# Interleaving two output pairs in the up projections of a two-layer decoder trunk

## The chip, the cores and the metric

One core of a Trainium2 chip runs the whole trunk in one launch. The metric is the device time of an execution in microseconds (us). Engines are named as in the profile: PE is TensorE, PEld its weight load, DVE VectorE, ACT ScalarE, POOL GpSimd, SP SyncE, which issues most DMAs.

## What is computed

A trunk of two layers over 1024 tokens of width 1024, in float32: layer 0 mixes with multi-head latent attention, layer 1 with a chunked gMLP unit. After each mixer comes a squared-ReLU MLP and then a gated per-layer embedding. What the change touches is the MLP and the last embedding step:

```python
hn = rms_norm(h, norm_ffn[i])
h = h + jnp.square(jax.nn.relu(hn @ ffn_w_up[i])) @ ffn_w_down[i]     # 1024 -> 4096 -> 1024
hn = rms_norm(h, norm_ple[i])
h = h + jax.nn.sigmoid(hn @ ple_w_gate[i]) * (p[i] @ ple_w_proj[i])   # gate 1024x1024, proj 256x1024
```

## The kernel before

**Numbers.** Every float32 operand of a matmul is split into a high and a low half (`split`, L110: a cast on ACT, L111, a subtraction on DVE, L112), and a product is three matmuls: high by high, high by low, low by high. All matmuls of the MLP have 512 columns.

**The up projection** (`wino_up`, L402) makes the 4096 output rows in 16 *pairs* of two 128-row blocks, and computes each pair by a Strassen-Winograd scheme over halves: seven products instead of eight, each of 12 matmuls (four k-blocks, three matmuls each), 84 in a pair. The seven products (`PRODUCTS`, L391) are numbered 0 to 6 here. Their left operands are combinations of four quarters of the weights (A12, A11, S1, S2, S4, S3, A22 in this order), made by `wino_weights` (L343): two loads of 512 KB (L350), four sums on DVE (L378 to L385) and seven splits. Their right operands are combinations of the normed input (B21, B11, T1, T2, B22, T3, T4), made by `NormX`; T3 and T4 are made late (L296, L302), inside the first pair.

Product 0 goes to a PSUM bank of its own (`y`), products 1, 3, 5 and 6 to bank `x`, products 2 and 4 to bank `z`; `x` and `z` are the halves of one two-bank tile `f0u4g` (pair 4 of layer 0). Between two products of a pair a bank is read out: copies on ACT (L446, L456, L463) and additions on DVE (L452, L466, L484). The finished half rows are then scaled by the norm's root with the ReLU (DVE, L478, L494, L502) and squared (ACT, L479, L495, L503), and each row of 1024 tokens goes to DRAM (`f_apark`, L522) as one store of 512 KB. In the first pair the three opening products run over k-blocks 0 to 2 before k-block 3, and the norm's sums and roots (L213, L222) are made there.

**What sets the order.** The program is a trace; a tile scheduler orders each engine's queue by trace order and by what it holds to be ready, and puts in the waits. Product 6 of a pair is written after product 0 of the next pair (`last`, L500), and each `prepare(n + 1)` puts one weight of the next pair into the trace. Buffers come from pools: `pr` (4 raw loads), `pw` and `ph` (8 each), `pt` (4), `phn` (32 tiles of 512 columns), `pa` (2 large tiles), `pb` (one of each tag), and PSUM as two two-bank tiles `g` and four banks `o`. A tile whose pool is full waits until an older one was used last, by a store too.

**Around it.** `up_first` (L595) starts the first pair's weights during the last steps of the matmul before it: `wo1` in layer 0, `go3` in layer 1. The down projection (`f0d`, `f1d`) follows the up projection. The last step `ple_out` (L846) goes over four blocks of 256 output columns and eight token blocks: 32 tiles of 30 matmuls with 256 columns each (6 for `p`, 24 for the gate), two transposes of `h` (L892), a sigmoid, a product and a sum (L904 to L906) and a store of 128 KB (L907). Its first weights are loaded inside the down projection's last sweep (`down_sweeps`, L607).

Of the kernel before, what the change touches and what calls it, by code (L numbers as in the profile page):

```python
# [16 lines left out]
P = 128  # L17
# [23 lines left out]
def trunk(ctx: ExitStack, tc: tile.TileContext, I, out):  # L41
# [129 lines left out]
    class Norm:  # L171
# [34 lines left out]
        def halve(self, c):  # L206
            acc = self.acc[:, CS[c]]
            shl = tmp(f"{self.name}{c}_shl", [P, 2, 512], F32R)
            self.last = S.copy(shl[:, 0], acc)
            V.tensor_tensor(shl[:, 1], acc, f32(shl[:, 0]), op=ALU.subtract)  # L210
            self.shl[c] = shl

        def sums(self, c, st):  # L213

            if c not in self.shl:
                self.halve(c)
            shl = self.shl[c]
            mm(st, onesr, shl[:, 0], True, False)
            mm(st, onesr, shl[:, 1], False, True)
            self.st[c] = st  # L220

        def roots(self, *chunks):  # L222
# [5 lines left out]
            for c in chunks:  # L228
# [3 lines left out]
                vr = tmp(f"{self.name}{c}_vr", [P, 2, 512])  # L232
# [27 lines left out]
    class NormX(Norm):  # L260
# [35 lines left out]
        def late_t3(self, q, h):  # L296
            t = tmp(f"{self.name}_{q}t3")[:, :512]
# [45 lines left out]
    def wino_weights(w, n):  # L343

        name = f"wx{cnt[0]}_"
        cnt[0] += 1
        raw = []
        for g in range(2):
            r = pr.tile([P, KT, P], F32, tag="raw", name=f"{name}r{g}")
            nc.sync.dma_start(r, w[:, (2 * n + g) * P:(2 * n + g + 1) * P].rearrange("(k p) f -> p k f", p=P))  # L350
            raw.append(r.rearrange("p (q e) f -> p q e f", e=2))
        quad = {f"A{g + 1}{e + 1}": raw[g][:, :, e, :] for g in range(2) for e in range(2)}
        count = [0]

        def new(what):
            m = 7 * n + count[0]
            count[0] += 1
# [8 lines left out]
        def sums(x):  # L366
            if n == 0 and x == "b":
                s = tmp(f"{name}s{x}", [P, 2, 4, P])
            else:
                pool, tag = (pb, "rb") if n == 0 else (ph, "h")  # L370
                s = pool.tile([P, 2, 4, P], F32, tag=tag, name=f"{name}s{x}")
            return s[:, 0], s[:, 1]

        def steps():
            yield put("A12", quad["A12"])
            yield put("A11", quad["A11"])
            s1, s2 = sums("a")
            V.tensor_tensor(s1, quad["A21"], quad["A22"], op=ALU.add)  # L378
            yield put("S1", s1)
            V.tensor_tensor(s2, s1, quad["A11"], op=ALU.subtract)  # L380
            yield put("S2", s2)
            s4, s3 = sums("b")
            V.tensor_tensor(s4, quad["A12"], s2, op=ALU.subtract)
            yield put("S4", s4)
            V.tensor_tensor(s3, quad["A11"], quad["A21"], op=ALU.subtract)  # L385
            yield put("S3", s3)
            yield put("A22", quad["A22"])

        return steps()

# [11 lines left out]
    def wino_up(w, F, nrm, first, h, nm, out, side):  # L402


        nfp = F // 256
        gens = {0: first[0], 1: wino_weights(w, 1)}
        made = {0: first[1]}

        def prepare(n):
            if n in gens:  # L410
                t = next(gens[n], None)
                if t is not None:
                    made.setdefault(n, []).append(t)

        def scale(u):
            for c in range(2):
                nrm.sums(c, pso(f"{u}st{c}"))
            nrm.roots(0, 1)

        def pair(n, late):  # L420
            u = f"{nm}{n}"
            if n + 2 < nfp:
                gens[n + 2] = wino_weights(w, n + 2)
            wt = made.setdefault(n, [])
            g = psg(f"{u}g")
            bank = {"x": g[:, CS[0]], "z": g[:, CS[1]], "y": pso(f"{u}y")}
            e0 = tmp(f"{u}e", [P, 2, 512])
            row = [tmp(f"{u}a0", [P, 2, 512])]

            def run(i, qs=range(4)):  # L430
                while len(wt) <= i:
                    prepare(n)
                c, b = PRODUCTS[i]
                product_x(bank[b], wt[i], nrm.x[c], i in OPENS, qs)

            if n == 0:
                for qs in (range(3), range(3, 4)):
                    for i in range(3):
                        run(i, qs)
                while len(wt) < 5:  # L440
                    prepare(0)
                for q in range(2):
                    nrm.late_t3(q, h)
            else:
                run(0)
            S.copy(e0[:, 0], bank["y"])  # L446
            if late is not None:
                late()
            prepare(n + 1)
            if n > 0:  # L450
                run(1)
            V.tensor_tensor(row[0][:, 0], bank["x"], e0[:, 0], op=ALU.add)  # L452
            if n > 0:
                prepare(n + 1)
                run(2)
            S.copy(e0[:, 1], bank["z"])  # L456
            if n == 0:
                for q in range(2, 4):
                    nrm.late_t3(q, h)
# [1022 lines left out]
```

## Time and profile before

| what | value |
|---|---|
| median of 3 runs | 2678.71 us (2677.26 to 2680.14) |
| the profiled execution | 2679.63 us, of which its span 2677.9 us |
| instructions | 34086 |
| granted TensorE clock, mean | 0.997 |

The profile is one execution. A row of the timeline has the start and duration in us, the engine, the line, the operation, its output and inputs, a count, and in brackets the idle time before it and what ended it. PE's matmuls are pipelined, so one shows as 0.39 us though the next starts 0.23 us after it. In the view of windows the count in brackets behind an engine's busy time is that of its instructions that touch the stretch.

### The profile page before, as it was taken

How to read it: one execution, taken by the hardware profiler on the slowest of the kernel's cores; microseconds unless marked ns; L12 is line 12 of the kernel's file. 1: busy time of each engine (PE TensorE's matmuls, PEld its weight loads, DVE VectorE, ACT ScalarE, POOL GpSimd, SP SyncE). 2: the span in 40 equal slices, each digit the busy share in tenths (PEclk: the TensorE clock that was granted, in tenths of full speed). 3: DMA queues.
4: the chain of work that ended last, by engine and by line, in shares of the span. 5: the costliest groups of instructions: out<-in, count | busy, mean ns of one | idle time of the engine just before them, and what ended most of it. 6: DMA issues, size and time to landing. Idle time of an engine off the chain costs nothing.

```text
span 2677.9 us, 34086 instructions
## 1 busy us (share of the span) xinstructions
PE 2618.7 (98%) x13216; PEld 2205.9 (82%) x13216; DVE 1479.2 (55%) x2398; ACT 1038.9 (39%) x2095; POOL 324.0 (12%) x460
## 2 busy tenths in 40 slices
PE   7999999999999999999999999999999999999999
PEld 7988888777777888888888787888677778888899
DVE  5777775975555434475522534437865654443642
ACT  4577772653443212164522312315643341221431
POOL 4544430000000000001211423020000000000000
PEclk9999999999999999999999999999999999999999
DMA  5200012242346323233233212212333363332221
GB/s 166 66 12 17 25 40 79 79 141 96 110 143 203 111 70 110 63 99 91 91 105 107 92 45 74 87 48 95 103 103 110 110 211 120 111 110 70 80 68 36
DMA packets 207026, 247.48 MB, mean 92 GB/s; under 512 B 9056, under 2 KB 168352, under 8 KB 206864
## 3 DMA queue, kind: packets, MB, share of 16 engines
q1 hardware_dynamic: 202048, 230.21, 26.4%
q0 software_dynamic: 4816, 15.10, 1.8%
q8 instruction: 104, 1.70, 0.3%
q14 instruction: 58, 0.48, 0.1%
HBM read 186.55 MB, written 58.72 MB: 92 GB/s over the span
## 4 chain that ended last, share of the span: by engine, by line
PE 85%; DVE 6%; ACT 3%; DMA 1%; issue 1%; POOL 0%; DVEq 0%; ACTq 0%; SPq 0%; POOLq 0%
PE f0d L65 13%; PE f1d L65 13%; PE vp L65 7%; PE go L65 6%; PE up L65 6%; PE e L65 4%; PE pg L65 3%; PE wo L65 3%; PE s L65 2%; PE pq L65 1%; PE av L65 1%; PE pj L65 1%; PE sv L65 1%; PE pk L65 1%; PE f1u9g L400 1%
## 5 line engine op out<-in xcount | busy, mean ns | idle before, releaser
L111 ACT CAST wh<-raw 128x1024 fp32r<-128x1024 f32 x96 | 101.0, 1052 | 386.1 <-PE f1d L65 135.1
L584 DVE TENSOR_TENSOR f0h<-f0d,f0h 128x512 f32<-128x512 f32 (+1 forms) x84 | 70.3, 865 | 157.1 <-PE f0d L65 157.1
L584 DVE TENSOR_TENSOR f1h<-f1d,f1h 128x512 f32<-128x512 f32 (+1 forms) x84 | 70.3, 865 | 155.5 <-PE f1d L65 155.5
L112 DVE TENSOR_TENSOR wl<-raw,wh 128x1024 fp32r<-128x1024 f32 x96 | 117.8, 1227 | 60.6 <-ACT wh L111 54.4
L659 POOL TENSOR_TENSOR f0h<-sig,f0h 128x512 f32<-128x512 f32 x16 | 21.9, 1388 | 856.9 <-DVE sig L658 838.2
L112 DVE TENSOR_TENSOR wx_A<-wx_r,wx_A 128x512 fp32r<-128x512 f32 x96 | 65.1, 688 | 80.2 <-ACT wx_A L111 79.9
L65 PE MATMUL go<-yl,wh 128*128 128x512 f32 x256 | 84.3, 395 | 2.8 <-DVE yl L112 2.8
L739 DVE BATCH_NORM_STATS2 vst<-vg 128x6 f32<-128x512 f32 (+1 forms) x40 | 23.4, 586 | 113.5 <-ACT vg L738 113.5
L65 PE MATMUL go<-yh,wh 128*128 128x512 f32 x256 | 84.5, 394 | 0.0
L65 PE MATMUL go<-yh,wl 128*128 128x512 f32 x256 | 83.0, 390 | 0.0
L809 ACT ACTIVATE u<-up,n_r 128x512 f32<-128x512 f32 x32 | 22.0, 688 | 156.6 <-PE up L65 156.6
L584 DVE TENSOR_TENSOR f0h<-go,f0h 128x512 f32<-128x512 f32 (+1 forms) x52 | 40.4, 809 | 66.2 <-PE go L65 66.2
L65 PE MATMUL s<-kT,q 128*128 128x512 f32 (+5 forms) x288 | 72.6, 354 | 2.4 <-DVE q L112 1.8
L738 ACT ACTIVATE vg<-vp,n_r 128x512 f32<-128x512 f32 (+1 forms) x40 | 24.0, 604 | 122.9 <-PE vp L65 121.4
L65 PE MATMUL av<-pt,v 128*128 128x256 f32 (+1 forms) x480 | 64.1, 284 | 5.3 <-DVE sm L1283 2.8
L65 PEld LDWEIGHTS av<-pt,v 128*128 128x128 f32 x480 | 59.9, 191 | 8.2 <-issue 3.8
L111 ACT CAST wx_A<-wx_r 128x512 fp32r<-128x512 f32 x96 | 58.4, 620 | 12.8 <-DVE wx_S L112 3.9
L1284 POOL TENSOR_SCALAR p<-p,sm 128x128 f32<-128x128 f32 (+3 forms) x64 | 49.5, 773 | 86.6 <-DVE sm L1283 54.3
L65 PEld LDWEIGHTS go<-yl,wh 128*128 128x128 f32 x256 | 48.4, 189 | 13.3 <-DVE yl L112 3.8
L65 PE MATMUL f0d<-f_ah,wh 128*128 128x512 f32 x192 | 59.2, 390 | 0.0
L65 PE MATMUL f1d<-f_ah,wh 128*128 128x512 f32 x192 | 59.2, 389 | 0.0
L65 PE MATMUL f0d<-f_al,wh 128*128 128x512 f32 x192 | 59.1, 389 | 0.0
(5251 smaller groups left out, 8154.0 us busy)
## 6 DMA issues: line engine op xcount, KB each, us to landing
wx_r<-in_ffn_w_up_dram SPq DMA_DIRECT2D x64, 512.0 KB, 4.1
raw<-in_ffn_w_down_dram SPq DMA_DIRECT2D x56, 512.0 KB, 3.4
f0ar<-f_apark SPq DMA_DIRECT2D x32, 512.0 KB, 3.5
f1ar<-f_apark SPq DMA_DIRECT2D x32, 512.0 KB, 3.4
raw<-in_ffn_w_down_dram SPq DMA_DIRECT2D x32, 256.0 KB, 3.0
raw<-in_ple_w_gate_dram SPq DMA_DIRECT2D x16, 512.0 KB, 4.0
vr<-vpark SPq DMA_DIRECT2D x16, 512.0 KB, 3.7
raw<-in_gmlp_w_out_dram SPq DMA_DIRECT2D x16, 512.0 KB, 3.3
```

Source lines behind the costliest of these rows:

```text
L65: PE.matmul(o, l, r, start=start, stop=stop)
L111: S.copy(hi, src)
L112: V.tensor_tensor(lo, src, f32(hi), op=ALU.subtract)
L400: PE.matmul(o, l, r, start=x, stop=y, skip_group_check=not first)
L584: V.tensor_tensor(h[j][:, c], u, h[j][:, c], op=ALU.add)
L659: G.tensor_tensor(h[j][:, cs], sg, h[j][:, cs], op=ALU.add)
L738: last = S.activation(t, o, AF.Gelu_apprx_tanh, scale=nrm.r[:, b:b + 1])
L739: V.bn_stats(vst[:, b, cc], t)
L809: S.activation(us[b][:, b % 2], o, AF.Gelu_apprx_tanh, scale=r[:, b:b + 1])
L1284: G.tensor_scalar(pr_[:, :n], pr_[:, :n], sm[:, 2:3], 1.0, op0=ALU.mult, op1=ALU.mult)
```

## The change

Two pairs, `a` and `b`, are now made together in a *double*; eight doubles replace 16 pairs, and the trace goes a0 b0 a1 b1 up to a6 b6. The order of PE's queue stays with the scheduler. A class `Up` replaces `wino_up`:

- Weights of a double are made alternately for `a` and `b`, at most 12 ahead of use (`both`); the four loads of the next double stand at the head of each double, in the first one after the norm's sums.
- Each finished half row of 512 tokens is scaled, squared and stored by itself: four stores of 256 KB for each pair.
- In the first double eight spare tiles (`spare`) hold weight sums, the two temporaries of T3 and the first half rows. In layer 0 they come from `phn`, beside B11, B21, T3 and T4 there; in layer 1 they are one `pa` tile, beside T3 and T4 there. T4's temporaries and the roots' room take the tag `acc`.
- The last step goes over two blocks of 512 columns: 16 tiles of 30 matmuls and four transposes, stores of 256 KB. Of its first five weight parts four stand in the trace inside the down projection's last sweep (three were whole there before), and the first block's gate takes all eight `pw` tiles instead of four.

```diff
-        def roots(self, *chunks):
+        def roots(self, *chunks, room=None):
...
-                vr = tmp(f"{self.name}{c}_vr", [P, 2, 512])
+                vr = room if room is not None else tmp(f"{self.name}{c}_vr", [P, 2, 512])
...
-        def late_t3(self, q, h):
-            t = tmp(f"{self.name}_{q}t3")[:, :512]
+        def late_t3(self, q, h, t):
...
         def new(what):
-            m = 7 * n + count[0]
-            count[0] += 1
+            m = 14 * (n // 2) + 2 * WORDER.index(what) + n % 2
...
+
+        def spare(self, x):
+
+            if self.parts is None:
+                if self.place is place0:
+                    self.parts = [phn.tile([P, 512], F32, tag="hn", name=f"{self.nm}sp{y}") for y in range(8)]
+                else:
+                    t = pa.tile([P, 8, 512], F32, tag="a", name=f"{self.nm}sp")
+                    self.parts = [t[:, y] for y in range(8)]
...
+        def room(self, n):
+            def take(x):
+                if n == 0 and x == "a":
+                    t = pb.tile([P, 2, 512], F32, tag="rb", name=f"{self.nm}s0a")
+                    s = [t[:, 0], t[:, 1]]
+                elif n < 2:
+                    o = 0 if n == 0 else 2 if x == "a" else 4
+                    s = [self.spare(o), self.spare(o + 1)]
+                else:
+                    t = ph.tile([P, 2, 512], F32, tag="h", name=f"{self.nm}s{n}{x}")
+                    s = [t[:, 0], t[:, 1]]
+                return [y.rearrange("p (q f) -> p q f", f=P) for y in s]
+            return take
...
+        def both(self, d):
+
+            a, b = 2 * d, 2 * d + 1
+            if d > 0 and len(self.made[a - 2]) + len(self.made[a - 1]) < 14:
+                a, b = a - 2, a - 1
+            if self.ready >= 12:
+                return
+            self.prepare(a if len(self.made.get(a, [])) <= len(self.made.get(b, [])) else b)
...
+            def scale(u):
+                for c in range(2):
+                    nrm.sums(c, pso(f"{u}st{c}"))
+                nrm.roots(0, 1, room=pb.tile([P, 2, 512], F32, tag="acc", name=f"{u}vr"))
...
+                def run(n, i, qs=range(4)):
+                    while len(self.made.get(n, [])) <= i:
+                        self.prepare(n)
+                    c, b = PRODUCTS[i]
+                    product_x(bank[n][b], self.made[n][i], nrm.x[c], i in OPENS, qs)
+                    if qs[-1] == 3:
+                        self.ready -= 1
+                        self.both(d + 1)
...
+                def finish(n, r, c, src=None):
+                    t = row[n][(r + c) % 2]
+                    V.scalar_tensor_tensor(t, t if src is None else src, 0.0, nrm.rb[:, CS[c]], op0=ALU.max, op1=ALU.mult)
+                    S.activation(t, t, AF.Square)
+                    out(2 * n + r, c, t)
...
+                def c11(n):
+                    if d == 0:
+                        row[n] = [self.spare(6 + n), None]
+                    else:
+                        t = tmp(f"{nm}{n}a", [P, 2, 512])
+                        row[n] = [t[:, 0], t[:, 1]]
+                    V.tensor_tensor(row[n][0], bank[n]["x"], e[n][:, 0], op=ALU.add)
+
+                def c12(n):
+                    if d == 0:
+                        row[n][1] = tmp(f"{nm}{n}a")[:, :512]
+                    V.tensor_tensor(row[n][1], bank[n]["z"], e[n][:, 0], op=ALU.add)
...
+                a, b = ns
+                if d == 0:
+                    for qs in (range(3), range(3, 4)):
+                        for i in range(3):
+                            for n in ns:
+                                run(n, i, qs)
+                    for k in range(6, KT):
+                        nrm.square(k, h)
+                    for c in range(2):
+                        nrm.halve(c)
+                    for n in ns:
+                        ycopy(n)
+                    for n in ns:
+                        c11(n)
+                        S.copy(e[n][:, 1], bank[n]["z"])
+                    for q in range(4):
+                        nrm.late_t3(q, h, self.spare(4 + q % 2))
+                    run(a, 3)
+                    scale(f"{nm}0")
...
+                    run(a, 0)
+                    ycopy(a)
+                    run(b, 0)
+                    ycopy(b)
+                    run(a, 1)
+                    c11(a)
+                    more()
+                    run(b, 1)
+                    c11(b)
+                    more()
+                    finish(a, 0, 0)
+                    run(a, 2)
+                    S.copy(e[a][:, 1], bank[a]["z"])
+                    more()
+                    finish(b, 0, 0)
+                    run(b, 2)
+                    S.copy(e[b][:, 1], bank[b]["z"])
...
+                S.copy(e[a][:, 0], bank[a]["x"])
+                if d > 0:
+                    more()
...
+                if d > 0:
+                    more()
+                run(a, 4)
+                c12(a)
...
+                if d == 0:
+                    for n in ns:
+                        finish(n, 0, 0)
+                    t = pb.tile([P, 2, 512], F32, tag="acc", name=f"{nm}t4")
+                    while len(self.made[b]) < 7:
+                        self.both(0)
+                    for q in range(4):
+                        nrm.late_t4(q, h, t[:, q % 2])
...
+                run(a, 5)
+                V.tensor_tensor(row[a][0], bank[a]["x"], e[a][:, 1], op=ALU.add)
...
+                run(b, 5)
+                V.tensor_tensor(row[b][0], bank[b]["x"], e[b][:, 1], op=ALU.add)
+                more(2)
+                finish(b, 1, 1)
+                run(a, 6)
+                finish(a, 1, 0, bank[a]["x"])
+                more(2)
+                side(d)
+                run(b, 6)
+                finish(b, 1, 0, bank[b]["x"])
...
+        def out(k, c, t):
+            nc.sync.dma_start(apark[k][:, CS[c]], t)
...
-        return gen, ready, after
+                up.load(0)
+            if j == 5:
+                up.load(1)
+            if j in (4, 5):
+                up.prepare(0)
+            if j == 6:
+                up.prepare(1)
+
+        return up, after
...
-                split(hi, lo, raw)
-                gt += [(hi[:, k], lo[:, k]) for k in range(4)]
...
+                both = [tmp(f"ewp{q}{x}", [P, 2, 512], F32R) for x in "hl"]
+            pj += load(both, wp, 0, 2, q * 512, f"ewp{q}")
+            yield pj, gt
+            if q:
+                whole = [pa.tile([P, KT, 512], F32R, tag="a", name=f"ewg{q}{x}") for x in "hl"]
+            for k0 in range(0, KT, 2):
+                if q:
+                    dst = [t[:, k0:k0 + 2] for t in whole]
+                else:
+                    dst = [pw.tile([P, 2, 512], F32R, tag="w", name=f"ewg{q}{k0}{x}") for x in "hl"]
+                gt += load(dst, wg, k0, 2, q * 512, f"ewg{q}{k0}")
+                yield pj, gt
...
+        first = weights(0)
+        for _ in range(4):
+            pj, gt = next(first)
         yield
+        next(first)
...
-                if q < 3 and b == 4:
-                    nw = weights(q + 1)
+                if q == 0 and b >= 3:
+                    nw = next(more)
...
+                o, oh = psg(f"e{q}{b}"), pso(f"eh{q}{b}")
+                og, op = o[:, :512], o[:, 512:]
...
-                for f in range(2):
-                    PE.transpose(oh[:, f * P:(f + 1) * P], h[2 * q + f][:, bs], idf)
+                for f in range(4):
+                    PE.transpose(oh[:, f * P:(f + 1) * P], h[4 * q + f][:, bs], idf)
...
-                t = tmp(f"et{q}{b}")[:, :256]
+                t = tmp(f"et{q}{b}")[:, :512]
...
-                nc.sync.dma_start(out[0, bs, q * 256:(q + 1) * 256], t)
+                nc.sync.dma_start(out[0, bs, q * 512:(q + 1) * 512], t)
```

## Rows read from the trace of the kernel before

**Rows 1.** The page, part 1 (busy time) and part 4 (chain), whole span.

```profile
PE 2618.7 (98%) x13216; PEld 2205.9 (82%) x13216; DVE 1479.2 (55%) x2398; ACT 1038.9 (39%) x2095; POOL 324.0 (12%) x460
...
PE 85%; DVE 6%; ACT 3%; DMA 1%; issue 1%; POOL 0%; DVEq 0%; ACTq 0%; SPq 0%; POOLq 0%
```

**Rows 2.** Windows, PE: inside f0d, then three stretches of each up projection.

```profile
core 0: us, PE busy (x), PEclk, DMA share, GB/s
880.00:1160.00 280.00, 280.00 (x1237) 1.00 0.28 90
...
505.60:560.00 54.40, 47.72 (x196) 1.00 0.29 91
...
560.00:800.00 240.00, 240.00 (x1028) 1.00 0.37 119
...
800.00:836.00 36.00, 35.38 (x152) 1.00 0.63 216
...
1873.20:1920.00 46.80, 41.10 (x169) 1.00 0.26 84
...
1920.00:2160.00 240.00, 239.14 (x1023) 1.00 0.36 114
...
2160.00:2203.00 43.00, 42.44 (x180) 1.00 0.69 234
```

**Rows 3.** Timeline, steady part, pair 4 of layer 0, between products 4 and 5.

```profile
606.68 3.00 PE L400 MATMUL f0u4g<-n1B,wx_S 128*128 128x512 f32 x12
609.52 0.39 PE L400 MATMUL f0u5y<-n1B212h,wx_A 128*128 128x512 f32 x1
609.72 0.69 DVE L466 TENSOR_TENSOR f0u4a<-f0u4g,f0u4e 128x512 f32<-128x512 f32 x1 [1.86 <-PE f0u4g L400]
610.20 0.39 PE L400 MATMUL f0u5y<-n1B213h,wx_A 128*128 128x512 f32 x1
610.47 0.19 PEld L400 LDWEIGHTS f0u4g<-n1T30h,wx_S 128*128 128x128 f32 x1 [0.30 <-DVE f0u4a L466]
610.47 0.50 PE L400 MATMUL f0u4g<-n1T30h,wx_S 128*128 128x512 f32 x1
610.81 0.40 PE L400 MATMUL f0u4g<-n1T30l,wx_S 128*128 128x512 f32 x1
```

**Rows 4.** Windows, all engines: the first 40 us of layer 0's up projection, one steady.

```profile
core 0: us, PE busy (x) PEld busy (x) DVE busy (x) ACT busy (x) POOL busy (x), PEclk, DMA share, GB/s
...
500.00:520.00 20.00, 19.46 (x87) 15.81 (x86) 19.80 (x31) 14.13 (x24) 0.00 (x0) 1.00 0.33 106
520.00:540.00 20.00, 16.49 (x65) 11.67 (x66) 19.86 (x32) 15.23 (x26) 0.00 (x0) 1.00 0.00 0
...
620.00:640.00 20.00, 20.00 (x87) 15.72 (x86) 12.02 (x19) 7.08 (x13) 0.00 (x0) 1.00 0.20 70
```

**Rows 5.** Timeline, DVE and PE in the first pair of layer 0.

```profile
513.79 0.69 DVE L112 TENSOR_TENSOR wx_A<-wx_r,wx_A 128x512 fp32r<-128x512 f32 x1
514.40 0.69 DVE L452 TENSOR_TENSOR f0u0a<-f0u0g,f0u0e 128x512 f32<-128x512 f32 x1
...
521.19 1.22 DVE L316 TENSOR_TENSOR n_acc<-n1sq,n_acc 128x1024 f32<-128x1024 f32 x1
522.33 0.69 DVE L112 TENSOR_TENSOR n1T40l<-f0u0t,n1T40h 128x512 fp32r<-128x512 f32 x1
...
530.10 0.50 PE L400 MATMUL f0u0g<-n1T42h,wx_A 128*128 128x512 f32 x1 [0.63 <-ACT n1T42h L111]
```

**Rows 6.** DMA issues: names, count, KB each, median us to landing.

```profile
wx_r<-in_ffn_w_up_dram SPq DMA_DIRECT2D x64, 512.0 KB, 4.1
...
vpark<-vg POOLq DMA_DIRECT2D x24, 256.0 KB, 2.3
...
out_dram<-et SPq DMA_DIRECT2D x32, 128.0 KB, 1.7
...
f_apark<-f0u4a SPq DMA_DIRECT2D x2, 512.0 KB, 2.8
```

**Rows 7.** The chain's last pieces: start us, us, what.

```profile
2655.37 3.60 PE e L65 x30
2659.19 3.58 PE e L65 x30
2662.99 3.60 PE e L65 x30
...
2666.59 0.22 PE e L892 x2
...
2673.52 0.48 ACT et L904
...
2674.55 0.42 DVE et L906
```

More of the change, by code (lines that the diff above doesn't have):

```diff
@@ L341, in place1, with wino_load @@
         return {"T1": halved, "T3": whole, "T4": whole}.get(c, single)(name, c, q)
[L343 to L345 removed]
+    def wino_load(w, n):
         cnt[0] += 1
@@ L364, in put @@
             return t
[L366 to L389, printed above, removed]
+        yield put("A12", quad["A12"])
+        yield put("A11", quad["A11"])
+        s1, s2 = room("a")
+        V.tensor_tensor(s1, quad["A21"], quad["A22"], op=ALU.add)
+        yield put("S1", s1)
+        V.tensor_tensor(s2, s1, quad["A11"], op=ALU.subtract)
+        yield put("S2", s2)
+        s4, s3 = room("b")
+        V.tensor_tensor(s4, quad["A12"], s2, op=ALU.subtract)
+        yield put("S4", s4)
+        V.tensor_tensor(s3, quad["A11"], quad["A21"], op=ALU.subtract)
+        yield put("S3", s3)
+        yield put("A22", quad["A22"])
+    WORDER = ["A12", "A11", "S1", "S2", "S4", "S3", "A22"]
     PRODUCTS = [("B21", "y"), ("B11", "x"), ("T1", "z"), ("T2", "x"), ("B22", "z"), ("T3", "x"), ("T4", "x")]
@@ L547, in side @@
         def side(n):
-            if n == FF // 256 - 1:
+            if n == FF // 512 - 1:
                 for _ in range(4):
                     rhs.append(next(gen[0]))
-        wino_up(up, FF, nrm, first, h0, f"f{i}u", out, side)
+        if True:
+            first.run(nrm, out, side, h0)
         cur = rhs[-1]
@@ L869, in ple_out, with load @@
-        nw = weights(0)
+        def load(dst, w, k0, nk, f0, name):
+            hi, lo = dst
+            raw = pr.tile([P, nk, 512], F32, tag="raw", name=f"{name}r")
+            nc.sync.dma_start(raw, w[k0 * P:(k0 + nk) * P, f0:f0 + 512].rearrange("(k p) f -> p k f", p=P))
+            split(hi, lo, raw)
+            return [(hi[:, k], lo[:, k]) for k in range(nk)]
+        def weights(q):
+            pj, gt = [], []
+            if q:
+                both = [pb.tile([P, 2, 512], F32R, tag=t, name=f"ewp{q}{t}") for t in ("acc", "rb")]
+            else:
+                both = [tmp(f"ewp{q}{x}", [P, 2, 512], F32R) for x in "hl"]
[4 more added lines that the diff above has]
+            for k0 in range(0, KT, 2):
+                if q:
+                    dst = [t[:, k0:k0 + 2] for t in whole]
+                else:
+                    dst = [pw.tile([P, 2, 512], F32R, tag="w", name=f"ewg{q}{k0}{x}") for x in "hl"]
+                gt += load(dst, wg, k0, 2, q * 512, f"ewg{q}{k0}")
+                yield pj, gt
@@ L870, in ple_out @@
+        first = weights(0)
+        for _ in range(4):
+            pj, gt = next(first)
         yield
+        next(first)
         nrm.tokens(0)
         pth, ptl = halves[i]
-        for q in range(4):
-            pj, gt = nw
+        for q in range(2):
+            if q == 0:
+                more = weights(1)
             for b in range(NB):
-                if q < 3 and b == 4:
-                    nw = weights(q + 1)
+                if q == 0 and b >= 3:
+                    nw = next(more)
@@ L1444, in trunk @@
     n4 = NormX("n4", gain(1, 1), place1)
-    gen, ready, after = up_first(I["ffn_w_up"][1])
+    up, after = up_first(1, place1)
     gmlp(h, n3, n4, after)
@@ L1449, in trunk @@
     last = ple_out(1, hf, n5)
-    ffn(1, n4, h, n5, lambda: next(last), (gen[0], ready), hf)
+    ffn(1, n4, h, n5, lambda: next(last), up, hf)
     next(last, None)
```

214 lines of the change are left out of this document (72 added, 142 removed).

## The prediction

> **What bounds the kernel now.** I began with the page: PE is busy 98% of the span and makes 85% of the chain that ended last, while DVE and ACT stand at 55% and 39% [rows 1]. So the change can give only what PE loses inside its busy time, or fewer PE cycles. To see that loss I counted matmuls in windows. Inside the down projection 1237 matmuls touch 280 us; two of them are edges, so one 512-column matmul costs 280/1235 = 0.2267 us, and a stretch of 240 us could hold 1060 in that view. The up projections hold 1028 and 1023 in such stretches, 196 where 54.4 us could hold 242, 169 where 46.8 us could hold 208, and 152 and 180 at the ends where 161 and 192 would fit [rows 2]. The lost time is therefore, for both layers together:
> - steady part: (32 + 37) x 0.2267 = 15.6 us,
> - first stretch: (46 + 39) x 0.2267 = 19.3 us,
> - last stretch: (9 + 12) x 0.2267 = 4.8 us.
>
> That is 39.7 us, the whole stock that the interleaving can draw on.
>
> The timeline shows how it is lost. After each product in `g` the next one waits until the bank is read out, even where it writes the other bank of the tile: product 5 of pair 4 (into `x`) starts 0.06 us after L466, which read `z`, has ended. PE bridges the time with single matmuls of the next pair's product 0, but it still loses 0.04 us before the wait and 0.11 behind it, where the starts lie 0.27 and 0.34 us apart instead of 0.2267 [rows 3]. Six such waits in a pair bound the loss at 0.9 us; the count gives 15.6 us over some 25 pairs, 0.6 each.
>
> **Steady part.** Nothing is removed from PE there: each pair keeps its 84 matmuls. What moves is the partner's product: it stands between a bank's read-out and the next product of the same pair, 12 x 0.2267 = 2.72 us. The read-out took 0.79 us from the end of the product's last matmul to the start of the next product [rows 3]. The slack is 1.9 us, or three DVE instructions of 512 columns, which follow each other in 0.61 us [rows 5]. DVE is busy 12.0 of 20 us there [rows 4], and the change leaves its work per pair nearly alone: one scaling of 1024 columns (1.14 us to the next start) becomes two of 512 (1.22) [rows 5], on a queue with room. Weights stay seven splits and four sums a pair. Two more stores per pair go to SP's queue, behind the loads of the next double; a half row's buffer is written again one product round (10.9 us, four products) after its last use, and a store of 256 KB lands in 2.3 us [rows 6], so this is covered; without that cover the first half row (c11) of the next double would wait for the store. Between no gain and the whole 15.6 us I take 13, as the one wait that is left out of reach is a read-out caught behind other DVE work. Bounds 6 and 15.6.
>
> **Last stretch.** The last pair has no successor to fill its waits; now it has a partner in every round. Of 4.8 us I take 3, bounds 1 and 4.8, since the reloads for the down projection, 216 to 234 GB/s there [rows 2], stay.
>
> **First double, the uncertain term.** DVE is busy 19.8 and 19.9 of 20 us there while PE drops to 65 matmuls in 20 us [rows 4], and PE waits for late operands (0.63 us for T4's k-block 2) [rows 5]. From the end of `wo1` (505.6) to the end of the first double DVE must still do, by the trace: four instructions for the last B and T tiles, two sums of h7 (1.2 us), 12 for S1 b, S2 b, S4 and S3, two squares' sums (1.14 us each), two halvings, two c11, eight for T3, four for the roots, two for A22, two for the next A12, two c12, two c21, six scalings, 12 for T4. That is 58 x 0.61 + 1.2 + 2.3 = 38.9 us. PE has 172 matmuls, 39.0 us, of its own, and 24 of the next double's product 0 to fill with (5.4 us). So neither engine is far ahead, and the loss is what their chain costs. Two waits are new. The four first products' k-block 3, then c11, T3 and the roots come in one block for both pairs: PE waits about 1 us at product 3 and 1 us at product 5. And T4's tiles find no room: in `phn` B11, B21, T3 and the eight spare tiles make 32, so T4's last k-block waits for the spare tiles 6 and 7, which hold the half rows until the store of b's second row has landed; in layer 1 the spare tiles are one `pa` tile, so all four k-blocks wait. Behind b's product 5 that chain is an addition 0.69, a scaling 0.69, a square (about 0.6, an estimate from the 0.48 of 256 columns [rows 7]), a store 2.3 [rows 6] and a split, some 5.5 us; in layer 1 three more k-blocks at about 1.2 us. In layer 0 a6 and b6 up to k-block 2 (18 matmuls, 4.1 us) and the 24 filler matmuls cover it, if the next A12 is there; its loads wait for raw buffers until A22 is split and land in 4.1 us [rows 6]. In layer 1 only the filler covers. I take 5 us lost in layer 0 and 7 in layer 1 against 19.3 now: a gain of 7.3 us. Bounds: all but 3 us gained (16), or 5 us more lost than now (-5).
>
> **Last step.** A tile of 256 columns repeats every 3.81 us, 3.60 of it 30 matmuls and 0.21 two transposes with their change-over [rows 7]. So a 256-column matmul costs 0.120 us and two of them 0.240, against 0.2267 for one of 512: each merged pair saves 0.0133 us, and 32 x 30 become 16 x 30. The new tile is 6.80 + 0.42 = 7.22 us against 7.62: 16 x 0.40 = 6.4 us less. At the end of the kernel a longer tail is bare: two DVE steps at 0.69 instead of 0.42 [rows 3, 7], a sigmoid some 0.2 us longer, a store of 256 instead of 128 KB, 2.3 instead of 1.7 [rows 6]: 1.3 us more. At the start of the step the first tile needs twice the gate columns, and two instead of four `pw` tiles are left to the sweep; a block there has 12 matmuls, 2.72 us, against a split of about 1.3 us, so I cost it at nothing, and at up to 4 us if the splits come late. Term 5.1, bounds 1 and 6.
>
> The rule against this term: [rows 2, 7] put the cost that does not depend on the columns at 0.0133 us a matmul. The Trainium skill, "TensorE: Matmul & The Clock Gate", section Back-to-back issue gap, gives a warm matmul its columns at 2.4 GHz plus about 2.5 ns. By that the 480 saved matmuls would give an estimated 1.2 us instead of 6.4, and the sum would end 5.2 us higher; the rows measure these very instructions and decide.
>
> **Sum.** 13 + 3 + 7.3 + 5.1 = 28.4 us. The rows are of an execution of 2679.6 us, 0.9 above the median, so the forecast is 2651.2. Adding the bounds gives 2637 (42.4 off) to 2677 (3 off).
>
> **Rivals.** *The waits stay* (the change doesn't do what it says). The scheduler may run a ahead of b, so that b only fills as the next pair does today, or read-outs may queue behind splits for more than 1.9 us. For it: the order is free, and PE takes single matmuls out of order today [rows 3]. Against it: it does so only when the earlier product isn't ready, and b's product is earlier in the trace. The steady gain falls from 13 to 2: 2662.
>
> *The first double grows* (slower). If both pairs' weight work goes ahead of T3 on a full DVE queue, product 5 starts only when DVE is through, 505.6 + 38.9 = 544.5. Then follow two products 5 (5.4), T4's chain (5.5, in layer 1 some 9.1), two products 6 (5.4), and no filler, because the next double's loads waited too and its first splits take 1.3 us: 562.1 in layer 0, 3.6 more in layer 1. Against 39.0 us of matmuls this loses 17.5 and 21.1 us; with the next double's sums and splits still to be made on the same full queue, 11 instructions a pair at 0.61 against two products of 2.72 us for their first use, another 8 us per layer. The loss is 54.6 instead of 12: 2694. It decides where the two first stretches lose over 45 us together. For it: DVE is full [rows 4]. Against it: T3 needs only ACT and DVE, and its turn comes before the roots.
>
> *Width saves nothing*: the cost of a matmul goes with its columns alone, so a wide one takes twice 0.120 us; the last step gives only its longer tail, -1.3 instead of 5.1: 2658. Against it: 0.2267 in the same kernel [rows 2, 7]. The Trainium skill's rule above comes close to this case.
>
> **Chances.** Forecast 0.71, waits stay 0.14, first double grows 0.10, width 0.05. What these executions can tell from no change is about 0.2%, 5.4 us: faster means under 2673.3, slower over 2684.1. The forecast and the waits together leave some 0.07 within it, where the first double takes back most of the gain: faster 0.83, same 0.07, slower 0.10. The range leaves out the slow rival and the best bound's corner: 2640 to 2674.
>
> **What would show it.** Right: over 1050 matmuls in 240 us of the steady parts; no wait of PE for L452's, L463's and L466's successors there; tiles of the last step 7.2 us apart. The first double is right if its first 55 us lose 5 to 7 us, with PE idle before T4 in layer 1. Wrong if the steady count stays near 1028, if the first stretches lose more than today's 19.3, or if the last step's first tile waits for gate weights.

## The result, and the profile after

The changed kernel takes **2662.7 us** (median of 5, 2661.7 to 2667.5) against 2680.1 for the kernel before (5 runs beside it, 2677.3 to 2681.7): a ratio of 0.9938, 95% interval 0.9928 to 0.9948. That is 17.5 us less, where the forecast had 28.4. It is faster and within the range, but 11 us of the expected gain did not come.

The execution that was profiled is the slowest of the five, 2667.5 us with a span of 2665.7. Against the span of before that is 12.2 us; the rest, up to 17.5, is variation between executions. Some of it can be seen: the stretch from the first product after `f0d` to the end of `go`, whose matmuls the change does not touch, took 694.6 us in this trace, 691.8 before, and between 689.8 and 693.8 in the kernels below.

The page of the changed kernel, parts 1 and 4, answers to [rows 1]:

```profile
PE 2600.9 (98%) x12736; PEld 2197.7 (82%) x12736; DVE 1482.0 (56%) x2396; ACT 1039.2 (39%) x2109; POOL 319.7 (12%) x460
...
PE 64%; DVE 3%; ACT 1%; DMA 1%; issue 0%; DVEq 0%; ACTq 0%; SPq 0%
```

PE has 480 instructions fewer, all from the last step, and is busy 17.8 us less. The chain's shares add up to 69% only, where they were 96%, so nothing is read from them here. The windows of PE answer to [rows 2]; the stretches start where `wo` and `go` end and are cut so that the first one takes in the whole first double.

```profile
core 0: us, PE busy (x), PEclk, DMA share, GB/s
506.80:566.00 59.20, 51.63 (x206) 0.91 0.30 94
566.00:806.00 240.00, 240.00 (x1060) 1.00 0.40 130
806.00:825.60 19.60, 19.50 (x87) 1.00 0.61 206
1870.90:1932.00 61.10, 53.24 (x217) 0.92 0.35 107
1932.00:2172.00 240.00, 239.19 (x1056) 1.00 0.40 128
2172.00:2190.00 18.00, 18.00 (x81) 1.00 0.59 199
```

Counted as in the prediction (length / 0.2267, plus two edges, less the matmuls seen):

- Steady part: 1060 and 1056 of 1060. 0.9 us is left of 15.6.
- Last stretch: 87 and 81 of 88.5 and 81.4. 0.4 us is left of 4.8.
- First stretches: 206 of 263 and 217 of 271.5, so 57 and 55 are missing. That is **25.4 us lost, where it was 19.3 and should have become 12**.

So the interleaving did nearly all it could where it runs freely, and the first double of each layer got worse. Its PE rows with a wait of over 2 us, layer 0 and then layer 1, from the timeline:

```profile
533.67 4.32 PE L392 MATMUL f0u0g<-n1B,wx_0S 128*128 128x512 f32 x12 [2.35 <-ACT f0u0e L543]
...
560.04 0.80 PE L392 MATMUL f0u0g<-n1T43l,wx_0A 128*128 128x512 f32 x1 [3.52 <-DVE n1T43l L112]
...
1897.34 0.80 PE L392 MATMUL f1u0g<-n4B220h,wx_0S 128*128 128x512 f32 x1 [2.35 <-ACT f1u0e L543]
...
1920.07 3.31 PE L392 MATMUL f1u0g<-n4T,wx_0A 128*128 128x512 f32 x6 [4.70 <-ACT n4T L111]
```

Two places, the same in both layers. **Ahead of T4** (product 6 of pair a) PE waits 3.52 and 4.70 us. How this wait is built up in layer 0 is seen on four engines, in the timeline around it:

```profile
546.08 0.39 PE L392 MATMUL f0u1g<-n1T33h,wx_1S 128*128 128x512 f32 x1
...
552.09 0.68 DVE L573 TENSOR_TENSOR f0usp<-f0u1g,f0u1e 128x512 f32<-128x512 f32 x1
...
552.26 5.23 SPq L596 DMA_DIRECT2D f_apark<-f0usp  x2
...
555.10 0.68 DVE L481 SCALAR_TENSOR_TENSOR f0usp<-f0usp,n_rb 128x512 f32<-128x512 f32 x1
...
556.51 0.63 ACT L482 ACTIVATE f0usp<-f0usp 128x512 f32<-128x512 f32 x1
...
559.31 0.68 DVE L112 TENSOR_TENSOR n1T43l<-f0ut,n1T43h 128x512 fp32r<-128x512 f32 x1
```

Product 5 of pair b ends at 546.3. Its addition reaches DVE 5.8 us later, at 552.1; the scaling comes 3.0 us behind that, the square at 556.5, the second of the two stores at 557.2 (the row's 5.23 us span two issues), and 2.1 us later T43's low half is written, by the program's order into the place of spare tile 7. PE goes on at 560.04, 13.7 us after the product.

In layer 1 the same links read:

```profile
1911.22 0.68 DVE L573 TENSOR_TENSOR f1usp<-f1u1g,f1u1e 128x512 f32<-128x512 f32 x1
...
1914.50 0.68 DVE L481 SCALAR_TENSOR_TENSOR f1usp<-f1usp,n_rb 128x512 f32<-128x512 f32 x1
...
1919.40 1.14 ACT L111 CAST n4T<-f1ut 128x512 fp32r<-128x512 f32 x2
```

Product 5 of pair b ends at 1909.8 there. The addition starts 1.4 us later, the scaling 2.6 us behind the addition's end, and T4's first split at 1919.40; PE goes on at 1920.07, 10.3 us after the product.

**Ahead of product 4** PE waits 2.35 us for the copy of the x bank, L543. ACT's timeline shows where that copy stands:

```profile
528.09 0.69 ACT L232 ACTIVATE n_rb<-f0u0st,epst 128x512 f32<-128x512 f32 x1
528.66 0.73 ACT L298 ACTIVATE f0usp<-h,gT 128x512 f32<-128x512 f32 x1
529.27 0.63 ACT L111 CAST n1T32h<-f0usp 128x512 fp32r<-128x512 f32 x1
529.78 0.71 ACT L235 ACTIVATE f0u0vr<-f0u0st,epst 128x512 f32<-128x512 f32 x1
...
531.40 0.70 ACT L232 ACTIVATE n_rb<-f0u0st,epst 128x512 f32<-128x512 f32 x1
531.98 0.65 ACT L237 ACTIVATE f0u0vr<-n_rb 128x512 f32<-128x512 f32 x1
532.49 0.65 ACT L236 ACTIVATE n_rb<-n_rb 128x512 f32<-128x512 f32 x1
533.01 0.60 ACT L543 COPY f0u0e<-f0u0g 128x512 f32<-128x512 f32 x1
```

ACT has no gap here. The product that the copy reads had ended by 528.6; the roots (L232 to L237) and T3's splits stand in front.

In the last step the chain has a tile of 30 matmuls every 7.29 us (forecast 7.22), and the last sweep of `f1d` has a wait that it did not have before. The chain (start us, us, what):

```profile
2589.09 6.84 PE e L65 x30
2596.36 6.86 PE e L65 x30
2603.65 6.84 PE e L65 x30
```

PE's timeline:

```profile
2533.96 0.73 PE L65 MATMUL f1d<-f_ah,wb 128*128 128x512 f32 x2 [0.93 <-DVE wb L112]
```

### The profile page after: what moved, and what is told of

Read it like the earlier page. It is cut to its first block, busy times and chain, and to the rows that moved or that the text cites. A ratio compares the mean times of both kernels' runs of the same rounds, so it can differ in the third digit from the quotient of the medians.

```text
span 2665.7 us, 33165 instructions
## 1 busy us (share of the span) xinstructions
PE 2600.9 (98%) x12736; PEld 2197.7 (82%) x12736; DVE 1482.0 (56%) x2396; ACT 1039.2 (39%) x2109; POOL 319.7 (12%) x460
## 3 DMA queue, kind: packets, MB, share of 16 engines
q1 hardware_dynamic: 206368, 230.21, 26.7%
## 4 chain that ended last, share of the span: by engine, by line
PE 64%; DVE 3%; ACT 1%; DMA 1%; issue 0%; DVEq 0%; ACTq 0%; SPq 0%
PE f0d L65 13%; PE f1d L65 12%; PE vp L65 7%; PE up L65 6%; PE go L65 5%; PE e L65 4%; PE pg L65 3%; PE pj L65 1%; PE sv L65 1%; PE f1u15g L392 1%; PE f1u14g L392 1%; PE f1u13g L392 1%; PE f1u12g L392 1%; PE f1u11g L392 1%; PE f1u10g L392 1%; PE f1u9g L392 1%
## 5 line engine op out<-in xcount | busy, mean ns | idle before, releaser
L1370 POOL TENSOR_SCALAR p<-p,sm 128x128 f32<-128x128 f32 (+3 forms) x64 | 49.3, 770 | 86.8 <-DVE sm L1369 54.6
L65 PE MATMUL f1d<-f_al,wh 128*128 128x512 f32 x192 | 59.2, 389 | 0.0
L65 PE MATMUL f0d<-f_ah,wl 128*128 128x512 f32 x192 | 59.1, 389 | 0.0
```

Of the source, the lines that this page charges most:

```text
L65: PE.matmul(o, l, r, start=start, stop=stop)
L1370: G.tensor_scalar(pr_[:, :n], pr_[:, :n], sm[:, 2:3], 1.0, op0=ALU.mult, op1=ALU.mult)
```

## The experiments

Each kernel was timed 4 to 11 times beside the kernel before (medians of 2678.6 to 2679.0 us in these groups). "Lost" below is PE's time in a stretch beyond 0.2267 us for each matmul started in it; for both layers' up projections together it is 39.3 us in the kernel before and 26.7 in the changed one.

### The first double's rows in tiles of their own

```diff
 def c11(n):
-    if d == 0:
-        row[n] = [self.spare(6 + n), None]
-    else:
-        t = tmp(f"{nm}{n}a", [P, 2, 512])
-        row[n] = [t[:, 0], t[:, 1]]
+    t = tmp(f"{nm}{n}a", [P, 2, 512])
+    row[n] = [t[:, 0], t[:, 1]]
...
 def c12(n):
-    if d == 0:
-        row[n][1] = tmp(f"{nm}{n}a")[:, :512]
...
-def scale(u):
+def add_up(u):
     for c in range(2):
         nrm.sums(c, pso(f"{u}st{c}"))
+
+def scale(u):
...
 for c in range(2):
     nrm.halve(c)
+add_up(f"{nm}0")
```

> The changed kernel, with the rows of each layer's first double in a tile of their own from the first half on (not in the spare tiles that T4 takes over), and the two sums of squares issued as soon as their halves are made. Store theory: T4's last k-block in layer 0 and all of T4 in layer 1 waited for the landing of a half row's store; without it PE's waits of 3.52 us (at 556.1) and 4.70 us (at 1915.0) ahead of T4 fall under 1 us each, and with the slow matmuls behind them the two first stretches lose about 5 us less each: 2662.7 - 9 = about 2653 to 2656. Rival, DVE's and ACT's own queues are what makes T4 late (DVE is busy without a break from 541 to 566): the waits shrink by less than a third, 2660 to 2663. Rival, the stretch loses the same in another place: the waits go and another of the same length comes ahead of the second double's first products, 2662.

Measured: **2650.5 us** (2648.1 to 2654.5), ratio 0.9895 (0.9881 to 0.9909). That is some 12 us under the changed kernel and within 1 us of the original forecast, 2651.2. PE's windows:

```profile
505.50:562.00 56.50, 51.23 (x222) 1.00 0.29 93
562.00:802.00 240.00, 240.00 (x1061) 1.00 0.42 136
...
1861.60:1918.00 56.40, 51.46 (x223) 1.00 0.29 94
1918.00:2158.00 240.00, 239.65 (x1058) 1.00 0.43 136
```

In the first stretches 29 and 28 matmuls are missing: 12.9 us lost instead of 25.4, where the prediction had 12. The waits ahead of T4 are gone altogether. T43 is split while b's addition, behind the last matmul of product 5, still waits for its turn on DVE:

```profile
542.63 0.39 PE L392 MATMUL f0u1g<-n1T33h,wx_1S 128*128 128x512 f32 x1
...
546.52 0.62 ACT L111 CAST n1T43h<-f0ut 128x512 fp32r<-128x512 f32 x1 [0.16 <-DVE f0ut L306]
...
547.61 0.69 DVE L112 TENSOR_TENSOR n1T43l<-f0ut,n1T43h 128x512 fp32r<-128x512 f32 x1
...
549.42 0.68 DVE L571 TENSOR_TENSOR f0u1a<-f0u1g,f0u1e 128x512 f32<-128x512 f32 x1
```

DVE is as full as in the changed kernel (busy 19.93 us from 541 to 561 in both), and the addition waits even longer, 6.6 us, yet T4 is on time. So the rival (DVE's and ACT's queues alone make T4 late) falls: T4 waited for the room.

### Its second edit alone

```diff
-def scale(u):
+def add_up(u):
     for c in range(2):
         nrm.sums(c, pso(f"{u}st{c}"))
+
+def scale(u):
...
     nrm.halve(c)
+add_up(f"{nm}0")
```

> Control for the run with the rows apart, which had a second edit: the changed kernel with only the sums of squares issued as soon as their halves are made, the rows still in the spare tiles. If the store theory holds for that run's whole gain, this is the changed kernel over again: 2661 to 2664, with waits of some 3.5 and 4.7 us ahead of T4. Rival, the early sums make rows and T4 early: 2654 to 2658.

Measured: 2663.7 us, ratio 0.9944 (0.9932 to 0.9957): the changed kernel over again, with 4.7 us of wait ahead of T4 in layer 1. The second edit by itself gives nothing. The rows' place by itself was not run, so it is not shown that it needs no help from the early sums.

### Roots behind the copies

```diff
 run(a, 3)
-scale(f"{nm}0")
 for n in ns:
     self.load(n + 2)
...
 S.copy(e[b][:, 0], bank[b]["x"])
 if d > 0:
     more()
+else:
+    scale(f"{nm}0")
```

> The changed kernel, with the sums of squares and the roots of the first double issued behind the two copies of the x bank, not ahead of them. Queue theory: product 4 waits for the copy of x, and that copy stands behind six operations of the roots in ACT's queue, 4.5 us after product 3's end; with the copies first the waits of 2.35 us at 531.2 and 1894.9 go, about 3 us each with the slow matmuls behind them: 2656 to 2658. Rival, the roots are needed just as much: the first rows are scaled later, their store and with it T4 come later by the same amount, and the wait ahead of T4 grows from 3.52 and 4.70 us to 5.5 and 7 us: 2662 to 2665.

Measured: 2658.5 us, ratio 0.9922 (0.9908 to 0.9936), 4.2 us under the changed kernel. Both theories had a part. The waits of 2.35 us are gone. In layer 0 the wait ahead of T4 shrank to 2.31 us, but waits of 1.35 and 1.23 us came ahead of the two products 6. In layer 1 the wait ahead of T4 grew by 1 us, as the rival said (PE's waits there: who waited for what, us in total, times, longest):

```profile
PE f1u0g L392 <- ACT n4T L111: 5.7, 1, 5.7
```

### Both together, and the weights held back as well

The first of the two kernels has both edits above. The second also issues none of the second double's weights until T4 is written:

```diff
 self.ready -= 1
-self.both(d + 1)
+if d > 0 or t4[0]:
+    self.both(d + 1)
...
 nrm.late_t4(q, h, t[:, q % 2])
+t4[0] = 1
```

> Both edits of the first two runs together: the first double's rows in tiles of their own, and the roots behind the copies of the x bank. Store and queue theories together: in the run with the rows apart, product 4 still waited for the copy of x (1.98 us lost at 529.6, 1.47 us at 1885.8); if nothing else is as late, these go too and the rest of the first run's gain stays: 2650.5 - 3 = 2646 to 2649. Rival, the roots set the end of the first double once the stores don't: later roots make the later rows and the banks of the second double late (1.23 to 1.36 us lost there four times already), and the gain is given back: 2650 to 2653.

> The run above, with none of the second double's weights issued until T4 is written. If DVE's queue (weights of the second double ahead of T4's blocks and of the rows that free the banks) holds the second double's first products, the four losses of 1.23 to 1.36 us there shrink and this is 2 to 4 us under the run above: 2643 to 2646. Rival, the weights are then late instead and the second double's first products wait for them: 2648 to 2655.

Measured: 2651.9 us, ratio 0.9903 (0.9888 to 0.9918), and 2652.4 us, ratio 0.9904 (0.9891 to 0.9918). Both came out as the rivals said: nothing on top of the first run. With the roots late, PE loses 16.2 us in the two up projections against 13.4 with the rows apart alone: the waits ahead of product 4 are gone, and others have come ahead of the products 6 (1.36 and 1.11 us in layer 0, 1.51 in layer 1), with up to 1.80 us for the scalings that free the second double's banks. With the weights late, the first double loses least of all (2.9 and 1.7 us up to its last product), and then PE waits in both layers for the third double's first weights, so that 17.1 us are lost in all (its wait in layer 0):

```profile
PE f0u4y L392 <- ACT wx_4A L111: 3.3, 1, 3.3
```

### Product 4 ahead of the copy of its x bank

To the rows apart, in the first double:

```diff
-S.copy(e[a][:, 0], bank[a]["x"])
-if d > 0:
+if d == 0:
+    run(b, 3)
+    for n in ns:
+        run(n, 4)
+        S.copy(e[n][:, 0], bank[n]["x"])
+        c12(n)
+else:
+    S.copy(e[a][:, 0], bank[a]["x"])
     more()
...
```

The doubles behind the first keep their order.

> The run with the rows apart, with product 4 of each pair of the first double issued ahead of the copy of its x bank (they use two halves of one tile, and the copy now waits for the product). Tile theory: product 4 waited for the copy because both name one tile, not because it needs it; the waits of 1.98 us at 529.6 and 1.47 us at 1885.8 go, the roots are no later than they were, and 2 to 3.5 us are gained on that run's 2650.5: 2647 to 2649. Rival, DVE sets the pace of the first double, as in the run with the roots moved: the same 3 us come back ahead of T3, T4 or the second double's banks, 2650 to 2652.

Measured: 2648.9 us, ratio 0.9887 (0.9874 to 0.9901); the interval overlaps that of the rows apart (0.9881 to 0.9909), so the times do not tell them apart. The trace does: the waits ahead of product 4 are gone, so they came from the tile that both banks share, yet PE loses 13.5 us in the up projections against 13.4. The loss has moved: in layer 0 product 6 of pair b now waits 0.96 us for the addition behind product 5, and the second double's first bank comes 1.80 us late in both layers, where it was 1.07 and 1.13. The tile theory holds for the wait, the rival for the time.

### The pairs of a double in turn

From the second double on all seven products of one pair are written, then all of the other, and the weights are made in that order too:

```diff
-            self.prepare(a if len(self.made.get(a, [])) <= len(self.made.get(b, [])) else b)
+            if d > 0 and a == 2 * d:
+                self.prepare(a if len(self.made.get(a, [])) < 7 else b)
+            else:
+                self.prepare(a if len(self.made.get(a, [])) <= len(self.made.get(b, [])) else b)
...
+                    for n in ns:
+                        run(n, 0)
+                        ycopy(n)
+                        run(n, 1)
+                        c11(n)
...
+                        run(n, 6)
+                        finish(n, 1, 0, bank[n]["x"])
```

> The changed kernel with the program of each double from the second on written pair after pair (all seven products of one, then all of the other), its weights made in that order too; stores, rooms and the last step as changed, and PE's order again the scheduler's. Interleaving theory: the waits of the steady part, 7.3 us in each layer before (1026 matmuls in 240 us) and none after, come from one pair's products following each other's copies; written in turn they come back, about +14: 2674 to 2680. Rival, the scheduler interleaves by itself as long as both pairs' banks and weights are free, and the order in the program is worth little: 2662 to 2667.

Measured: 2680.8 us, ratio 1.0007 (0.9998 to 1.0016): no faster than the kernel before, and 18 us over the changed one. Its steady windows:

```profile
566.00:806.00 240.00, 239.58 (x1023) 1.00 0.38 121
1932.00:2172.00 240.00, 240.00 (x1025) 1.00 0.37 116
```

Those are nearly the counts of [rows 2] again (1028 and 1023), where the changed kernel has 1060 and 1056. In each window PE's weight loads (PEld) wait over 0.15 us 50 times for a read-out of a bank (56 or 57 times in the kernel before) and never for a weight's split; in the changed kernel they wait once in both windows together. By this it is the products' order that counts, and not the weights'. PE's order is the scheduler's here too: that freedom by itself is worth nothing; the order of the program is.

### The last step alone, taken out and put in

The first kernel is the changed one with the function `ple_out` of before, the second the kernel before with the `ple_out` of the change.

> The changed kernel with the last step of before (weights in blocks of 256 columns). The forecast had the 512-column step at +5.1 us net (16 tiles x 0.40 = 6.4 less a tail of 1.3), and the trace after shows 1.1 us lost in f1d's last sweep behind the weights' splits and a tail 1.3 us longer: so 2662.7 + 4 = 2665.5 to 2668, and f1d's last sweep without the wait of 0.93 us. Rival, the width saves nothing because the steps are bound by the matmuls' columns: 2661 to 2663.

> The kernel before with the new last step alone. If the parts of the change add up, this one gains what the run above loses: 2680.1 - 4 = 2674 to 2677. Rival, the gain of the last step comes from the order of PE that the interleaving leaves to the scheduler, or nothing comes of it: 2679 to 2681.

Measured: 2666.4 us, ratio 0.9952 (0.9940 to 0.9965), against 0.9938 with the new step, so the step is worth about 3.8 us there, though these two intervals overlap; and 2675.5 us, ratio 0.9987 (0.9978 to 0.9996), so 3.5 us here. Within that spread the parts add up. In `old_last` PE waits for nothing in `f1d`'s last sweep; in `new_last` the 1.1 us are lost there as in the changed kernel.

### Weights and tail of the last step

```diff
-for _ in range(4):
+for _ in range(3):
     pj, gt = next(first)
 yield
-next(first)
+for _ in range(2):
+    next(first)
...
+w = 256 if q == 1 and b == NB - 1 else 512
+for f0 in range(0, 512, w):
...
```

These two edits were put on three kernels: on the one with both edits (rows and roots; "the first of these four" in the text below), on the one with product 4 moved, and on the rows apart alone. In the last two the halves of the last tile are two tiles.

> The first of these four, with the last step's last tile finished in two halves of 256 columns, and one block of its gate weights loaded after f1d's last sweep instead of ahead of it. Tail theory: from PE's last matmul to the end 6.0 us against 4.7 before, about 0.8 to 1 us of it from the tile's double width; and the wait of 0.93 us in the last sweep comes from the splits of those weights: together 1 to 2 us under the first of these four, 2645 to 2647. Rival, the end is the store's own time and the sweep waits for its own weights: no difference.

> The run above, with one block of the last step's gate weights loaded after f1d's last sweep, and the last tile finished in two halves of separate tiles (in one tile, the second half's sigmoid stood 0.49 us behind the first half's product on DVE, and the tail got only 0.2 us shorter). Sweep 1.9 us by the run that had it, tail 0.6: 2.0 to 2.5 us under the run above, 2645 to 2649. Rival, the tail is the store's: 1.5 to 1.9 under it.

> The run with the rows apart, with the last step's two edits of the run above and product 4 where it was. By the terms measured so far: 2650.5 - 2.3 = 2648 to 2649; whichever of this and the run above is lower tells whether product 4's place is worth anything. Rival, nothing is left to gain behind f1d's last sweep: 2650 to 2651.

Measured: with the roots moved, 2650.4 us (ratio 0.9895, 0.9881 to 0.9908); with product 4 moved, 2648.3 us (0.9889, 0.9875 to 0.9902); on the rows apart alone, **2647.4 us** (0.9886, 0.9871 to 0.9902), the lowest median of all. That is 1.5, 0.6 and 3.1 us under the kernels that the edits were put on, but each interval overlaps that of the kernel without the edits, and the three overlap each other: the times don't show the gain. In the traces the wait in the sweep is gone, and from the end of `go` to PE's last matmul it is 781.4 us instead of 783.3, 780.1 instead of 782.6, and 781.2 instead of 782.3. The tail, from the start of PE's last matmul to the end, barely moved, from 6.0 to 5.8 us, also where the halves have two tiles of their own for the result. There too the second half's sigmoid stands behind the first half's product on DVE (timeline of the last kernel):

```profile
2640.53 0.42 DVE L991 TENSOR_TENSOR et<-e,et 128x256 f32<-128x256 f32 x1 [5.59 <-ACT et L990]
...
2640.99 0.47 ACT L990 ACTIVATE et<-e,n_r 128x256 f32<-128x256 f32 x1 [0.49 <-DVE et L991]
```

Both read the PSUM tile `e`. That this tile is the reason was not tried.

So the version to take is the changed kernel with the rows of the first double in tiles of their own and one weight block of the last step loaded after the sweep. With the last tile in halves as well, as it was measured, it is some 31 us, 1.1%, under the kernel before (2647.4 against 2679.0) and about 15 us under the changed one; without the halves it was not run.

## Why the prediction was right, and where it was not

| term | forecast, us | measured, us | from |
|---|---|---|---|
| steady part | 13 | 14.7 | windows |
| last stretch | 3 | 4.4 | windows |
| first double | 7.3 | -6.1 | windows |
| last step | 5.1 | 3.8 | run without it |
| sum | 28.4 | 16.8 | times: 17.5 |

The whole came out within its range, 2640 to 2674, though one of its four terms has the wrong sign.

**Steady part and last stretch: right**, and a little small. The slack of 1.9 us behind each product was enough for every read-out but one, a wait of 0.81 us in layer 1. The cause is shown by taking the interleaving away: 2680.8 us.

**First double: the waits named, the size wrong by 13.4 us.** The forecast was a gain of 7.3 us with bounds of 16 and -5; measured are 6.1 us more lost than before, outside the bounds. The prediction named the wait ahead of T4 and its cause: T4's last k-block in layer 0 and the whole of T4 in layer 1 wait for a store out of the spare tiles. The step that failed is the length of that chain, "some 5.5 us" behind b's product 5, which the filler was to cover. It added up the bare durations: addition, scaling, square, store, split. Measured it was 13.7 us in layer 0 and 10.3 in layer 1, so that PE stood still for 3.52 and 4.70 us. Most of the difference is queueing on DVE: in layer 0 5.8 us before the addition's turn and 2.3 between its end and the scaling, in layer 1 1.4 and 2.6. That share is read from the trace; no run gave the links an earlier turn. The same prediction had read DVE as busy 19.9 of 20 us in the kernel before [rows 4] and used that for the engine's total, but not for the wait of each link.

Two more things were missed. The prediction had a wait of about 1 us at product 5, for the roots among others; there is none. The roots stood in ACT's queue ahead of the copy that product 4 waits for, and that cost 2.35 us in each layer. With the roots behind the copies this wait went and the time fell by 4.2 us, but on top of the first cure it brought nothing. And the matmuls behind the long waits ran at half the clock, 5.2 us for which there was no term (last section).

That the kernel with the rows apart took 2650.5 us against a forecast of 2651.2, and lost 12.9 us in the first stretches against 12, is luck. The 12 us were to hold T4's chain, in layer 1 by the prediction's own figures 9.1 us less 5.4 of filler, and in that kernel nothing waits ahead of T4. What it loses, both layers together, is 2.5 us at product 3, where about 2 were forecast, 3.1 at product 4, and 4.6 at the banks of the second double, which wait for the scalings (L483) and for which the prediction had no term; the rest is slower starts right behind these waits.

**The rivals.** The first double did not grow as the slow rival had it (54.6 us lost, deciding from 45), but at 25.4 us it did pass the prediction's own mark for being wrong, "more than today's 19.3". *The waits stay* has the right time, 2662, by the wrong way: the steady waits went and others came. *Width saves nothing* is refuted by the tiles of the last step, which would then come 7.62 us apart and come 7.29 apart; the two runs of 3.5 and 3.8 us agree.

**Last step: 1.3 us too large.** The tiles come 7.29 us apart instead of 7.62, so 16 x 0.33 = 5.3 us; the tail is 1.3 us longer, as forecast (6.0 against 4.7 from the start of the last matmul to the end). The start of the step was costed at nothing, with up to 4 us if the splits come late; it cost the 1.1 us lost in `f1d`'s last sweep. A wait of 0.89 us for `et` in the old last step, which the term did not count, is gone: 5.3 - 1.3 - 1.1 + 0.9 = 3.8. The 0.2267 and 0.120 us of [rows 2, 7] decided rightly. The Trainium skill, "TensorE: Matmul & The Clock Gate", section Back-to-back issue gap, gives a warm matmul its columns at 2.4 GHz plus about 2.5 ns, by which 480 matmuls fewer would save an estimated 1.2 us. The 5.3 us of this trace don't agree with it.

## What to carry to other kernels

When a change lets a buffer be reused, price the release as a chain in its queues: each link waits for its turn, and on an engine that is full the turns can cost more than the work (here, in layer 0, 13.7 us for 5.5 of durations). Before interleaving two streams, look for operands of the first round whose room is freed only by the last work of the same round, a store above all, and give that work a place of its own; here this small edit was worth some 12 us, nearly as much as the interleaving had brought net. Where a corrected kernel then lands on the forecast, compare the terms before calling the forecast right. And after one wait is cured, look for what is late next before counting the second cure: three further edits in the first double moved their waits and brought nothing on top of the first that the runs can tell.

## What the runs showed of the hardware

The waits cost more than their length. Behind each of the waits of 2.35 to 4.70 us PE's granted clock fell to half, the 1.2 GHz level. Behind the one ahead of product 4 in layer 0 that came after some 1.5 us of matmuls that still start about 0.23 us apart; in layer 1 the window from 1897.4 to 1900.1 has 0.50. Two windows of the changed kernel, behind the waits ahead of T4 in layers 0 and 1:

```profile
560.00:566.00 6.00, 5.45 (x12) 0.52 0.79 225
1920.00:1923.50 3.50, 3.42 (x7) 0.50 0.95 265
```

Matmuls start 0.43 us apart there instead of 0.2267. The changed kernel's up projections have 26 such matmuls, 26 x 0.20 = 5.2 us of the 25.4 lost. The kernel before has none, its waits in the first stretches being 1.1 us at most, and the one with the rows apart has none, with a longest wait of 1.8 us; the one with rows and roots has seven in a row in layer 1, behind two waits of 1.5 and 1.8 us that end 7.7 us apart. The prediction had no term for this, though the trace of before shows it in another place: behind a wait of 4.43 us ahead of `sv`, at 1486, seven matmuls of `up` start 0.43 us apart.

The Trainium skill, "TensorE: Matmul & The Clock Gate", section Wait — 56ns, not 53.3ns?, gives 426.7 ns from start to start for a matmul of 512 columns at the lower clock; the 0.43 us of this trace agree.
